# Band transposes over three PSUM banks, one block's output norm moved into the output projection, and token rows squared on the chip instead of loaded again

## The chip, the cores and the metric

The kernel runs on one core of a Trainium2 chip. The metric is the device time of one execution in microseconds (us). The kernel before has a median of 3063.79 us over three runs (3062.14 to 3065.21).

## The reference

One layer of a hybrid streaming encoder, in float32, over 2048 prompt tokens and 32 sample tokens (`T` = 2080 together), 1024 channels each. Cut to what matters here:

```python
a = rmsnorm(x, g_attn)                       # mean of x*x over the 1024 channels
qa, ka, va, qb, kb, vb = split(a @ w_in)     # group A: 4 heads, group B: 8 heads of 64
oa = diff_attn(qa, ka, va)                   # two softmax maps, w = p1 - lam * p2
ob = band_attn(qb, kb, vb)                   # a chunk of 64 sees itself and 8 chunks before
oa = rmsnorm_per_head(oa, subln_g) * (1 - lam_init)
ob = rmsnorm(ob, out_norm_b)                 # over the 512 channels of group B
h = x + concat(oa, ob) @ w_out
c = rmsnorm(h, g_mlp)
h = h + square(relu(c @ w_up)) @ w_down
h = h + sigmoid(h @ w_ple_gate) * (p @ w_ple_proj)
y = rmsnorm(h, g_final)
```

New keys and values of both groups are outputs too.

## The kernel before, in words

Every float32 operand of a large product is split into a high and a low part (`split`, lines 178 to 187), and `mm3` (lines 215 to 221) makes one product of three matmuls on TensorE (PE). So a group of 8 terms is 24 matmuls into one PSUM bank, which ScalarE (ACT) or VectorE (DVE) then empties ("evicts").

The tokens are cut into blocks b = 0 to 3 of 512, 512, 512 and 544 columns. The program is written as generators that are woven together, and a scheduler puts each engine's instructions into one fixed order when the program is built. Each engine then works through its own order, waiting wherever its next instruction isn't ready. All loads and stores are issued by one queue (SP), in order too. The written order of the first third is:

1. `prep` of blocks 0 and 1 beside the group A values (`vtile`, `vps`). For every 128 tokens `prep` loads the tokens transposed (`xt`, from `x_t`), multiplies by the gain, splits into `aH` and `aL`, loads the same tokens a second time as rows (`x`), squares these on ACT with a sum along the row (line 385), and makes the norm factor `r` from the sum (`rsqrt`). The values are scaled with `r` as they leave PSUM (`vraw`, line 427). `prep` of blocks 2 and 3 comes later, beside projections.
2. Group A queries and keys of blocks 0 and 1 (`proj`, `qps`), then the differential attention `attn_a` of the first half of the tokens, with the group B projections of all blocks as work to fill in.
3. Band attention `attn_b` of the first half (`JB[:2]`), 64 steps of 128 queries (8 heads, 4 pairs, 2 tiles each). A full step is four score matmuls `sb`, five transposes `tpb` of the softmax row, and three output matmuls `ob` (six for each pair of tiles); the first 32 steps see fewer keys and have two `sb`. Between `sb` and `tpb` lie additions and a maximum on DVE, an exponential on ACT, a reciprocal on DVE and a scaling on ACT. After `tpb`, ACT and DVE split the result into `pb`, which `ob` needs. Projections of blocks 2 and 3 in groups B and A (`proj_a`) are the filler here.
4. Band attention of the second half. Beside `proj_a`, `onorm` of blocks 0 and 1 is woven in: for each it loads the four band output tiles `oT` (`oraw`, a ring of three, tag `tmp`), squares and adds them (`sqacc`), sums over partitions with two matmuls (`css`, lines 1046 and 1047), makes the norm factor `r`, and stores it in DRAM (`rB`, line 1058).
5. `oload(0)`: eight raw tiles of block 0 are loaded through the same ring of three, tiles 4 to 7 are multiplied by `r`, which is loaded back from `rB` (`rb`, line 899), and all are split into the operands `oact` of the output projection.
6. The differential attention of the second half, then `outproj(0)` (`ops`, lines 918 to 925, eight steps d of eight terms) with `oload(1)` woven in, one tile for each d, then `outproj(1)`, then the MLP of blocks 0 and 1 (`ups`, `dps`) and so on.

PSUM has eight banks. Two (`mz`, tag `mm`) and a third (pool `mmx`) form the ring `mm` of the projections; `ps_s` has two for scores, `ps_t` two for transposes, `ps_o` one for outputs.

Of the kernel before, what the change touches and what calls it, by code (L numbers as in the profile page):

```python
# [20 lines left out]
P = 128  # L21
D = 1024
# [56 lines left out]
ONP = (28, 1, 6)  # L79
ONQ = (8, 1, 1)  # L80
PW = 272


def drain(gen):
    for _ in gen:
        pass
# [57 lines left out]
class Kern:  # L144
# [89 lines left out]
        eng.tensor_tensor(out, y0, v, op=ALU.mult)  # L234
        return out

    def xsrc(self, t0, n):
        a = self.a
        if t0 < SP:
            return a["x_prompt"][0, t0 : t0 + n, :]  # L240
        return a["x_sample"][0, t0 - SP : t0 - SP + n, :]

    def consts(self, cp):
        nc, a = self.nc, self.a
        self.ident = cp.tile([P, P], F32, name="ident")
        make_identity(nc, self.ident)
        ones = cp.tile([P, P], F32, name="ones")
        nc.gpsimd.memset(ones, 1.0)
        self.ones = cp.tile([P, P], F32R, name="ones_r")
        nc.vector.tensor_copy(self.ones, ones)  # L250

        def cols(name, ap, k):
            t = cp.tile([P, k], F32, name=name)
# [110 lines left out]
    def prep(self, b, acts, pp, mm, tag, first=None):  # L364
        nc = self.nc
        aH, aL = acts[b]
        late = []
        for i, (c0, n) in enumerate(toks(b)):
            t0 = 512 * b + c0
            xt = pp.tile([P, 8, P], F32, tag="xt", name="xt")  # L370
            self.dma(xt[:, :, :n], self.xT[:, :, t0 : t0 + n])
            if first is not None:
                first()
                first = None
            x = pp.tile([P, D], F32, tag="x", name="x")
            self.dma(x[:n], self.xsrc(t0, n))
            m = 2 if b == 0 and i == 0 else 1
            for k in range(0, 8, 8 // m):
                ks = slice(k, k + 8 // m)
                xg = xt[:, ks, :n]  # L380
                g = self.g_attn[:, ks].unsqueeze(2).broadcast_to([P, 8 // m, n])
                nc.vector.tensor_tensor(xg, xg, g, op=ALU.mult)
                self.split(aH[:, ks, c0 : c0 + n], aL[:, ks, c0 : c0 + n], xg, "act", "dve")
            st = pp.tile([P, 1], F32, tag="st", name="st")
            nc.scalar.activation(x[:n], x[:n], AF.Square, accum_out=st[:n])
            r = self.rcol[:n, 4 * b + i : 4 * b + i + 1]
            self.rsqrt(pp, st[:n], 1, 1.0 / D, EPS, nc.vector, "r1", n, out=r)

            def spread(r=r, c0=c0, n=n):
                nc.tensor.transpose(rp[:, c0 % 512 : c0 % 512 + n], r.broadcast_to([n, P]), self.ident[:n, :n])  # L390
# [474 lines left out]
        self.dma(t, self.oT[:, k, t0 : t0 + n])  # L865
        return t

    def onorm(self, b, wk, ps, tag, dst):
        nc = self.nc
        n, t0 = BN[b], 512 * b  # L870
        sq = wk.tile([P, BLK], F32, tag="acc", bufs=2, name="sqacc")[:, :n]
        for k in range(4, 8):
            raw = self.raw_o(wk, k, t0, n)
            if k == 4:
                nc.scalar.activation(sq, raw, AF.Square)
            else:
                nc.scalar.activation(raw, raw, AF.Square)
                self.pool_tt(sq, sq, raw, ALU.add)
        yield from self.colnorm2(sq, b, 1.0 / 512, wk, ps, tag, dst, [])

    def oload(self, b, wk, up, out):
        nc = self.nc
        n, t0 = BN[b], 512 * b
        if isinstance(up, tuple):
            oact = up[0].tile([P, 8, n], F32R, tag="h", name="oact")
            oact = [
                [oact[:, k] for k in range(8)],
                [up[1].tile([P, up[1].aw], F32R, tag="u", name="ou") for _ in range(8)],
            ]
        elif up.whole:  # L890
            oact = [up.tile([P, 8, up.aw], F32R, tag="act", name="oact") for _ in range(2)]
            oact = [[t[:, k, :n] for k in range(8)] for t in oact]
        else:
            oact = [[up.tile([P, up.aw], F32R, tag="u", name="ou")[:, :n] for k in range(8)] for _ in range(2)]
        out[b] = oact
        for k in range(8):
            if k == 4:
                r = wk.tile([P, BLK], F32, tag="r", bufs=2, name="rb")[:, :n]
                self.dma(r, self.rB[:, t0 : t0 + n])
            raw = self.raw_o(wk, k, t0, n)  # L900
            if k >= 4:
                nc.vector.scalar_tensor_tensor(
                    raw, raw, self.g_b[:, k - 4 : k - 3], r, op0=ALU.mult, op1=ALU.mult
                )
            self.split(oact[0][k], oact[1][k], raw, "act", "dve")
            yield
# [473 lines left out]
    def run(self):  # L1380
        tc, nc, a = self.tc, self.nc, self.a
        with ExitStack() as top:
# [91 lines left out]
            for js in JB[len(JB) // 2 :]:  # L1474
                self.attn_b(js, bp, ps_s, ps_t, ps_o)

            def proj_a():
                yield from self.proj(HALVES[1], 0, acts, sg, mm, gs=range(GS))
                for b in HALVES[1]:
                    yield from self.proj((b,), 0, acts, sg, mm, vs=(), gs=range(GS, 4))  # L1480
# [178 lines left out]
```

## Time and profile before

| | |
|---|---|
| median of three runs | 3063.79 us (3062.14 to 3065.21) |
| the profiled execution | 3069.65 us |
| its span | 3067.9 us |
| granted TensorE clock, mean | 0.985 |
| busy share PE, DVE, ACT, POOL | 96%, 60%, 57%, 62% |
| bytes moved by DMA | 529.54 MB, 173 GB/s over the span |

The profiled execution lies 5.86 us (0.19%) above the median of the timed runs, and its span is 1.75 us shorter than its time. PE is the busiest engine, so time is to be found where PE is not busy or where its clock is below 1.

### The profile page before, as it was taken

The page shows a single profiled execution, that of the slowest core. Times are in us where ns is not written, and L with a number is a line of the kernel's source. Part 1 is how long each engine was busy: PE and PEld are TensorE (multiplying, and loading weights), DVE is VectorE, ACT ScalarE, POOL GpSimd, SP SyncE. Part 2 cuts the span into 40 slices and gives each one's busy share as a digit, 9 for nine tenths or more (in the row PEclk, how much of TensorE's full clock was granted, in tenths as well). Part 3 has the DMA queues.
Part 4 walks back from the last instruction along what each step waited for, and adds up shares of the span by engine and source line. Part 5 has one row for each costly group of instructions (what it writes and reads, how often), then busy time and mean ns, then how long its engine had stood idle before and what let it go on. Part 6 is the DMA issues. An engine that isn't in the chain of part 4 may idle for free. (4 is left out here: it accounts for less than half of the span.)

```text
span 3067.9 us, 50404 instructions
## 1 busy us (share of the span) xinstructions
PE 2947.2 (96%) x17409; PEld 2599.0 (85%) x17409; DVE 1830.6 (60%) x4233; ACT 1746.5 (57%) x3234; POOL 1887.9 (62%) x2509
## 2 busy tenths in 40 slices
PE   7999999899789999999999999999899999999997
PEld 6788889899677888888888888879798888999997
DVE  5156554654655555566666565545677885577664
ACT  5256554765666666566666565554555545555455
POOL 3467775324146544656655565777688888787774
PEclk9999999999899999999999999999999999999999
DMA  9878866976687554455655543347433446333331
GB/s 310 250 222 245 241 221 211 262 228 211 190 248 241 147 148 131 145 155 172 198 149 155 150 128 125 118 148 249 136 131 117 148 151 231 122 101 112 102 99 57
DMA packets 298119, 529.54 MB, mean 173 GB/s; under 512 B 36668, under 2 KB 161632, under 8 KB 297864
## 3 DMA queue, kind: packets, MB, share of 16 engines
q1 hardware_dynamic: 297864, 526.32, 55.6%
q8 instruction: 138, 2.26, 0.3%
q14 instruction: 117, 0.96, 0.1%
HBM read 425.19 MB, written 104.97 MB: 173 GB/s over the span
## 5 line engine op out<-in xcount | busy, mean ns | idle before, releaser
L176 POOL TENSOR_TENSOR wl<-wr,wh 128x256 fp32r<-128x256 f32 x648 | 492.8, 792 | 270.2 <-ACT wh L181 230.7
L181 ACT ACTIVATE piece<-wr 128x512 fp32r<-128x512 f32 x406 | 245.8, 625 | 290.4 <-PE ups L220 133.3
L176 POOL TENSOR_TENSOR piece<-wr,piece 128x256 fp32r<-128x256 f32 x404 | 338.0, 863 | 92.3 <-ACT piece L181 85.2
L181 ACT ACTIVATE wh<-wr 128x1024 fp32r<-128x1024 f32 x228 | 240.5, 1055 | 190.8 <-PE ups L220 45.9
L166 POOL TENSOR_TENSOR wl<-wr,wh 128x256 fp32r<-128x256 f32 x264 | 202.9, 799 | 208.4 <-ACT wh L181 202.6
L219 PE MATMUL dps<-uh,piece 128*128 128x272 f32 (+1 forms) x768 | 247.0, 325 | 8.3 <-ACT piece L181 5.0
L221 PE MATMUL dps<-uh,piece 128*128 128x272 f32 (+1 forms) x768 | 247.3, 325 | 1.1 <-POOL piece L166 0.9
L220 PE MATMUL dps<-ul,piece 128*128 128x272 f32 (+1 forms) x768 | 248.1, 324 | 0.1
L166 POOL TENSOR_TENSOR piece<-wr,piece 128x256 fp32r<-128x256 f32 x280 | 235.1, 872 | 18.9 <-ACT piece L181 15.4
L219 PE MATMUL ups<-cs,piece 128*128 128x256 f32 (+1 forms) x864 | 246.2, 285 | 0.0
L221 PE MATMUL ups<-cs,piece 128*128 128x256 f32 (+1 forms) x864 | 246.1, 285 | 0.0
L220 PE MATMUL ups<-cs,piece 128*128 128x256 f32 (+1 forms) x864 | 245.9, 285 | 0.0
L219 PE MATMUL qps<-aH,wh 128*128 128x512 f32 (+1 forms) x640 | 226.9, 355 | 2.0 <-DVE ql L475 2.0
L220 PE MATMUL qps<-aL,wh 128*128 128x512 f32 (+1 forms) x640 | 227.9, 356 | 0.0
L221 PE MATMUL qps<-aH,wl 128*128 128x512 f32 (+1 forms) x640 | 226.5, 354 | 0.0
L1112 DVE TENSOR_TENSOR h<-h,dps 128x512 f32<-128x512 f32 x256 | 173.5, 682 | 80.2 <-PE dps L221 77.0
L638 ACT ACTIVATE e<-e,nm 128x128 f32<-128x128 f32 (+16 forms) x136 | 157.2, 1156 | 108.5 <-DVE nm L636 108.0
L1155 DVE TENSOR_TENSOR h<-h,dps 128x272 f32<-128x272 f32 (+1 forms) x384 | 189.0, 514 | 42.9 <-PE dps L221 42.3
L219 PE MATMUL dps<-uh,wh 128*128 128x512 f32 x512 | 205.7, 402 | 0.6 <-DVE h L1112 0.6
L219 PE MATMUL ups<-cH,wh 128*128 128x512 f32 x512 | 202.5, 396 | 0.0
L221 PE MATMUL ups<-cH,wl 128*128 128x512 f32 x512 | 202.2, 395 | 0.1
L220 PE MATMUL ups<-cL,wh 128*128 128x512 f32 x512 | 202.0, 394 | 0.0
(307 smaller groups left out, 9234.0 us busy)
## 6 DMA issues: line engine op xcount, KB each, us to landing
wr<-w_up SPq DMA_DIRECT2D x128, 512.0 KB, 3.5
wr<-w_down SPq DMA_DIRECT2D x128, 512.0 KB, 3.6
v<-vSa SPq DMA_DIRECT2D x64, 512.0 KB, 4.6
q<-qS SPq DMA_DIRECT2D x128, 256.0 KB, 5.2
wr<-w_qk SPq DMA_DIRECT2D x50, 512.0 KB, 5.2
ka<-kS SPq DMA_DIRECT2D x32, 512.0 KB, 7.1
wr<-w_out SPq DMA_DIRECT2D x32, 512.0 KB, 4.8
wr<-w_ple_gate SPq DMA_DIRECT2D x32, 512.0 KB, 3.5
```

The lines of the kernel that those rows point to most:

```text
L166: nc.gpsimd.tensor_tensor(out[:, sl], a[:, sl], b[:, sl], op=op)
L176: nc.gpsimd.tensor_tensor(out[:, sl], a[:, sl], b[:, sl], op=op)
L181: nc.scalar.activation(hi, raw, AF.Copy)
L219: nc.tensor.matmul(ps, lh, rh, start=start and i == 0, stop=False)
L220: nc.tensor.matmul(ps, lh, rl, start=False, stop=False)
L221: nc.tensor.matmul(ps, ll, rh, start=False, stop=stop and i == n - 1)
L638: nc.scalar.activation(row, row, AF.Exp, bias=nmx, accum_out=z[:nr, m : m + 1])
L1112: nc.vector.tensor_tensor(hv, hv, ps, op=ALU.add)
L1155: nc.vector.tensor_tensor(hv, hv, ps, op=ALU.add)
```

## The change: three edits to the first third of the program

**Transposes.** For the first half of the band attention the transposes `tpb` take their PSUM tile from a ring `tb` of three banks, the two of `ps_t` and the third bank `third`. The projections that run there (`proj` of blocks 2 and 3, `prep(3)`, `proj_a`) have the two banks of `mz` left. The second half of the band attention, and everything else that uses `mm`, is as before.

**Output norm.** `onorm(1)` is taken out of the weave with `proj_a`. Its two steps run inside `outproj(0)`, at d = 3 and d = 5, and `oload(1)` follows from d = 5 on, three tiles for each d. Its four raw tiles come in one load of 1 MB (`oraws`) into room of the pool that later holds `h`. For blocks 0 and 1 `r` stays in SBUF (`ro`); it isn't stored to `rB` and loaded again.

**Tokens.** The rows `x` are not loaded. The product with the gain goes to a tile of its own (`xg`), ACT squares `xt` in place, DVE adds up the eight channel groups (`sk`, reading with a step of 128 elements), and one matmul with a column of ones (`sp`) finishes the sum.

```diff
@@ def consts
+        self.one = ones[:, :1]
@@ def prep
-            x = pp.tile([P, D], F32, tag="x", name="x")
-            self.dma(x[:n], self.xsrc(t0, n))
+            xg = pp.tile([P, 8, P], F32, tag="xg", name="xg")
             m = 2 if b == 0 and i == 0 else 1
             for k in range(0, 8, 8 // m):
                 ks = slice(k, k + 8 // m)
-                xg = xt[:, ks, :n]
                 g = self.g_attn[:, ks].unsqueeze(2).broadcast_to([P, 8 // m, n])
-                nc.vector.tensor_tensor(xg, xg, g, op=ALU.mult)
-                self.split(aH[:, ks, c0 : c0 + n], aL[:, ks, c0 : c0 + n], xg, "act", "dve")
-            st = pp.tile([P, 1], F32, tag="st", name="st")
-            nc.scalar.activation(x[:n], x[:n], AF.Square, accum_out=st[:n])
+                nc.vector.tensor_tensor(xg[:, ks, :n], xt[:, ks, :n], g, op=ALU.mult)
+                self.split(aH[:, ks, c0 : c0 + n], aL[:, ks, c0 : c0 + n], xg[:, ks, :n], "act", "dve")
+            nc.scalar.activation(xt[:, :, :n], xt[:, :, :n], AF.Square)
+            sk = pp.tile([P, P], F32, tag="sk", name="sk")[:, :n]
+            nc.vector.tensor_reduce(sk, xt[:, :, :n].rearrange("p k c -> p c k"), axis=AX.X, op=ALU.add)
+            sp = mm.tile([P, 512], F32, tag=tag, name="sp")
+            nc.tensor.matmul(sp[:n, :1], sk, self.one, start=True, stop=True)
             r = self.rcol[:n, 4 * b + i : 4 * b + i + 1]
-            self.rsqrt(pp, st[:n], 1, 1.0 / D, EPS, nc.vector, "r1", n, out=r)
+            self.rsqrt(pp, sp[:n, :1], 1, 1.0 / D, EPS, nc.vector, "r1", n, out=r)
@@ def onorm
-    def onorm(self, b, wk, ps, tag, dst):
+    def onorm(self, b, wk, ps, tag, dst, out=None, room=None):
...
+            room, sq = room
+            sq = sq.tile([P, sq.aw], F32, tag="u", name="sqacc")[:, :n]
+            room = room.tile([P, 8, n], F32, tag="h", name="oraws")[:, :4]
+            self.dma(room, self.oT[:, 4:8, t0 : t0 + n])
         for k in range(4, 8):
-            raw = self.raw_o(wk, k, t0, n)
+            raw = self.raw_o(wk, k, t0, n) if room is None else room[:, k - 4]
...
-        yield from self.colnorm2(sq, b, 1.0 / 512, wk, ps, tag, dst, [])
+        yield from self.colnorm2(sq, b, 1.0 / 512, wk, ps, tag, dst, [] if out is None else out)
@@ def oload
-            if k == 4:
+            if k == 4 and r is not None:
+                r = r.pop()
+            elif k == 4:
                 r = wk.tile([P, BLK], F32, tag="r", bufs=2, name="rb")[:, :n]
                 self.dma(r, self.rB[:, t0 : t0 + n])
@@ the program
-            mm = Rings((mz, "mm"), (mz, "mm"), (opened(mmx, "mmx", 1, PSUM), "mm"))
+            third = opened(mmx, "mmx", 1, PSUM)
+            mm = Rings((mz, "mm"), (mz, "mm"), (third, "mm"))
...
+            tb = Rings((ps_t, "tp"), (ps_t, "tp"), (third, "mm"))
             for js in JB[: len(JB) // 2]:
-                self.attn_b(js, bp, ps_s, ps_t, ps_o)
-            weave(self.proj((2,), 1, acts, sg, mm), lifted(self.prep(3, acts, pp, mm, "mm")), 3)
+                self.attn_b(js, bp, ps_s, tb, ps_o)
+            weave(self.proj((2,), 1, acts, sg, mz), lifted(self.prep(3, acts, pp, mz, "mm")), 3)
...
-            drain(self.proj((3,), 1, acts, sg, mm))
+            drain(self.proj((3,), 1, acts, sg, mz))
...
-            weave2(proj_a(), [self.onorm(b, wq, mm, "mm", self.rB) for b in HALVES[0]], ONP)
+            ro = {b: [] for b in HALVES[0]}
+            weave2(proj_a(), [self.onorm(0, wq, mm, "mm", None, ro[0])], ONP)
...
-            drain(self.oload(0, wq, actq, oa))
+            drain(self.oload(0, wq, actq, oa, ro[0]))
...
-            weave(self.outproj(0, wk, oa[0], mm, acc[0]), self.oload(1, wk, (hq, uq), oa), 1, 0, OW)
+            g = self.onorm(1, wk, mm, "mm", None, ro[1], (hq, uq))
+            for i, _ in enumerate(self.outproj(0, wk, oa[0], mm, acc[0])):
+                if i in (O1, O2):
+                    next(g, None)
+                if i == O2:
+                    g = self.oload(1, wk, (hq, uq), oa, ro[1])
+                if i >= O2:
+                    for _ in range(O3):
+                        next(g, None)
+            drain(g)
```

In `proj_a` the ring `mm` becomes `mz` too; `O1, O2, O3 = 3, 5, 3`.

The scheduler makes a new order of this. The first place is TensorE at the last projection matmul (`qps`). Of before, in the order of the engine, with the line ahead and the shape behind:

```order
L221 MATMUL qps<-aH,wl 128x272
L1046 MATMUL css<-sh,ones_r 128x512
L1047 MATMUL css<-sl,ones_r 128x512
L804 MATMUL sb<-kbt,q 128x320 x4
L856 MATMUL ob<-pb,vbt 128x512 x4
L856 MATMUL ob<-pb,vbt 128x2x128
L826 MATMUL tpb<-ident,eb 128x128 x4
```

The last `qps` stands behind 176 `sb` of the band attention. From there full steps of four `sb` follow one another with nothing between them, until the first matmul of the output projection, behind 224 `sb`. These are the rows there, also of before:

```order
L804 MATMUL sb<-kbt,q 128x320 x4
L826 MATMUL tpb<-ident,eb 128x128 x4
L219 MATMUL ops<-oact,wh 128x512 x2
L826 MATMUL tpb<-ident,eb 128x128
L220 MATMUL ops<-oact,wh 128x512
```

So twelve full steps stand without a matmul of other work. The same two places of the changed kernel fit into one piece of the order of TensorE:

```order
L823 MATMUL tpb<-ident,eb 128x128 x5
L221 MATMUL qps<-aL,wh 128x272
L222 MATMUL qps<-aH,wl 128x272
L1051 MATMUL css<-sh,ones_r 128x512
L1052 MATMUL css<-sl,ones_r 128x512
L801 MATMUL sb<-kbt,q 128x320 x4
L853 MATMUL ob<-pb,vbt 128x512 x4
L853 MATMUL ob<-pb,vbt 128x2x128
L823 MATMUL tpb<-ident,eb 128x128 x4
L853 MATMUL ob<-pb,vbt 128x2x128
L823 MATMUL tpb<-ident,eb 128x128
L220 MATMUL ops<-oact,wh 128x512 x2
```

Now the last `qps` stands behind 240 `sb`, 16 full steps later than before, and the first `ops` behind 244: the output projection follows one step behind the last projection. The first 36 `ops` use raw tiles 0 to 3 of three steps d, which need no norm. The first `ups` of the MLP stands behind 296 `sb` before and behind 316 now, which is five full steps.

The second place is the queue SP at the start of the program, first of before:

```order
L157 DMA xt<-x_t 128x8x128
L157 DMA g_attn_s<-g_attn 128x8
L157 DMA x<-x_prompt 128x1024
L157 DMA wr_142<-w_v 128x1024
L157 DMA wr_151<-w_v 128x1024
```

and of the changed kernel:

```order
L158 DMA xt<-x_t 128x8x128
L158 DMA g_attn_s<-g_attn 128x8
L158 DMA wr_144<-w_v 128x1024
L158 DMA wr_153<-w_v 128x1024
L158 DMA xt<-x_t 128x8x128
```

The loads of weights and of the next tokens move up by the loads of rows, 17 in all. On DVE 17 instructions `sk` are new, on TensorE 17 matmuls `sp`. From about 2050 us of the profile on, the orders of PE and DVE are the same.

More of the change, by code (lines that the diff above doesn't have):

```diff
@@ L81 @@
 PW = 272
+O1, O2, O3 = 3, 5, 3
 def drain(gen):
@@ L235, in rsqrt @@
         return out
[L237 to L241, printed above, removed]
     def consts(self, cp):
@@ L866, in raw_o @@
         return t
-    def onorm(self, b, wk, ps, tag, dst):
+    def onorm(self, b, wk, ps, tag, dst, out=None, room=None):
         nc = self.nc
         n, t0 = BN[b], 512 * b
-        sq = wk.tile([P, BLK], F32, tag="acc", bufs=2, name="sqacc")[:, :n]
+        if room is None:
+            sq = wk.tile([P, BLK], F32, tag="acc", bufs=2, name="sqacc")[:, :n]
+        else:
+            room, sq = room
+            sq = sq.tile([P, sq.aw], F32, tag="u", name="sqacc")[:, :n]
+            room = room.tile([P, 8, n], F32, tag="h", name="oraws")[:, :4]
+            self.dma(room, self.oT[:, 4:8, t0 : t0 + n])
         for k in range(4, 8):
-            raw = self.raw_o(wk, k, t0, n)
+            raw = self.raw_o(wk, k, t0, n) if room is None else room[:, k - 4]
             if k == 4:
@@ L878, in onorm, with oload @@
                 self.pool_tt(sq, sq, raw, ALU.add)
-        yield from self.colnorm2(sq, b, 1.0 / 512, wk, ps, tag, dst, [])
-    def oload(self, b, wk, up, out):
+        yield from self.colnorm2(sq, b, 1.0 / 512, wk, ps, tag, dst, [] if out is None else out)
+    def oload(self, b, wk, up, out, r=None):
         nc = self.nc
@@ L1477, in proj_a @@
             def proj_a():
-                yield from self.proj(HALVES[1], 0, acts, sg, mm, gs=range(GS))
+                yield from self.proj(HALVES[1], 0, acts, sg, mz, gs=range(GS))
                 for b in HALVES[1]:
-                    yield from self.proj((b,), 0, acts, sg, mm, vs=(), gs=range(GS, 4))
-            weave2(proj_a(), [self.onorm(b, wq, mm, "mm", self.rB) for b in HALVES[0]], ONP)
+                    yield from self.proj((b,), 0, acts, sg, mz, vs=(), gs=range(GS, 4))
+            ro = {b: [] for b in HALVES[0]}
+            weave2(proj_a(), [self.onorm(0, wq, mm, "mm", None, ro[0])], ONP)
             s12.close()
@@ L1630 @@
     arrays["ck_t"] = np.ascontiguousarray(np.stack(ck).transpose(0, 3, 2, 1)).reshape(2, P, 512)
-    arrays["x_t"] = columns(arrays["x_prompt"][0], arrays["x_sample"][0])
+    arrays["x_t"] = columns(arrays.pop("x_prompt")[0], arrays.pop("x_sample")[0])
     arrays["p_t"] = columns(arrays.pop("p_prompt")[0, 0], arrays.pop("p_sample")[0, 0])
```

## The prediction

> **What bounds the kernel now.** I read the shares of the engines first, then windows over the stretches that the change touches, then what TensorE (PE) waits for, then single waits in the timeline.
>
> ```profile
> PE 2947.2 (96%) x17409; PEld 2599.0 (85%) x17409; DVE 1830.6 (60%) x4233; ACT 1746.5 (57%) x3234; POOL 1887.9 (62%) x2509
> ```
>
> PE is busy 2947.2 of 3067.9 us, so the kernel's time is PE's work plus its gaps and slow stretches. The windows (length, then busy time and count of PE, PEld, DVE, ACT, POOL, then PE's granted clock, the DMA share and GB/s) show where these lie:
>
> ```profile
> 0.00:50.00 50.00, 27.68 (x175) 25.32 (x175) 33.29 (x64) 33.26 (x72) 27.98 (x35) 0.97 1.01 348
> 50.00:100.00 50.00, 49.78 (x312) 42.77 (x313) 20.16 (x70) 19.83 (x53) 3.69 (x6) 0.97 0.70 221
> 130.00:170.00 40.00, 40.00 (x170) 32.28 (x169) 4.75 (x7) 8.24 (x11) 22.15 (x32) 0.98 0.67 219
> 520.00:773.00 253.00, 242.79 (x1690) 227.04 (x1689) 132.12 (x496) 160.18 (x359) 90.44 (x150) 0.99 0.80 233
> 773.00:825.40 52.40, 35.29 (x149) 26.46 (x148) 29.16 (x109) 33.91 (x71) 7.26 (x15) 0.77 0.66 192
> 825.40:965.00 139.60, 126.09 (x606) 103.54 (x606) 80.40 (x224) 85.44 (x161) 68.22 (x99) 0.97 0.83 241
> 1000.00:1200.00 200.00, 200.00 (x1015) 167.75 (x1014) 107.35 (x361) 131.94 (x263) 97.29 (x149) 1.00 0.51 148
> ```
>
> Three stretches stand out: the start; 773 to 825.4 us (PE at 67% and clock 0.77), between the last `qps` and the first `ops`; and the output projection behind it. What PE works on is counted by tile: `ops` in 825.4:965, then `sb`, `ups` and `dps` in 1000:1200.
>
> ```profile
> 825.40:965.00 139.60, 98.16 (x383) 0.97 0.83 241
> 1000.00:1200.00 200.00, 27.21 (x128) 1.00 0.51 148
> 1000.00:1200.00 200.00, 75.57 (x300) 1.00 0.51 148
> 1000.00:1200.00 200.00, 82.47 (x326) 1.00 0.51 148
> ```
>
> **Two prices.** In 130:170 PE does 170 matmuls of 512 columns without a gap, 40/170 = 0.235 us each (the durations of single ones overlap, so I use the spacing). In 1000:1200 it is full too: 626 such matmuls of the MLP and 128 `sb`, which at four each are 32 full band steps. A step that runs beside filler thus costs PE (200 − 626 × 0.235)/32 = 1.65 us.
>
> In 773:825.4 there are only the twelve full steps that the order shows without other work: 12 × 1.65 = 19.8 us of work in 52.4 us. 32.6 us are lost, since a step alone is a chain through DVE and ACT. In 825.4:965 there are 383 `ops`, 90.0 us, and 18 steps, 29.7 us: 119.7 of 139.6, 20 us lost.
>
> Why does the output projection start only at 825.4? The timeline of ACT, SP and PE just before it (start, duration, engine):
>
> ```profile
> 817.84 0.46 SPq L157 DMA_DIRECT2D oT<-t  x1
> 820.09 1.28 SPq L157 DMA_DIRECT2D oraw<-oT  x3
> 822.80 0.63 ACT L877 ACTIVATE oraw<-oraw 128x512 f32<-128x512 f32 x1 [1.13 <-DMA oraw<-oT]
> 824.52 1.14 ACT L181 ACTIVATE oact<-oraw 128x512 fp32r<-128x512 f32 x2
> 825.46 1.20 PE L219 MATMUL ops<-oact,wh 128*128 128x512 f32 x2
> ```
>
> Block 1's norm squares its last raw tile (L877) at 822.8, which could only be loaded after the last head's store `oT<-t` at 817.84. Block 0's raw tiles use the same ring of three and the same queue, so they stand behind it: block 0 waits for block 1.
>
> **Change 1 and 2, the middle of the program.** Taking `onorm(1)` out ahead of `oload(0)` removes that wait, and the new order puts `ops` one step behind the last `qps`. That `qps` itself stands 16 full steps later, as transposes have a third bank and projections one less. From 520 to 965 us it was 253 + 52.4 + 139.6 = 445 us. Now the first stretch holds 16 more steps, 16 × 1.65 = 26.4; one step follows, 1.65; then a wait T for block 0's norm; and the output projection sees five steps fewer before the first `ups` than the same point did, −8.25. 253 + 26.4 + 1.65 + T + 139.6 − 8.25 = 412.4 + T, a gain of 32.6 − T.
>
> T: the chain from `css` to the operands, as it was before:
>
> ```profile
> L1046 PE MATMUL css<-sh,ones_r x1: 394/394/394, 773.2 to 773.2; 128*128 128x512 f32 x1
> L157 SPq DMA_DIRECT2D rB<-r x1: 319/319/319, 784.2 to 784.2; - x1
> L902 DVE SCALAR_TENSOR_TENSOR oraw<-oraw,g_b_s,rb x8: 722/752/762, 835.1 to 911.2; 128x512 f32<-128x512 f32 x8
> L181 ACT ACTIVATE oact<-oraw x16: 613/624/636, 783.7 to 911.9; 128x512 fp32r<-128x512 f32 x16
> L187 DVE TENSOR_TENSOR oact<-oraw,oact x8: 669/678/694, 825.2 to 845.9; 128x512 fp32r<-128x512 f32 x8
> ```
>
> `r` is there 11.0 us after `css`; scaling and splitting tile 4 take 0.75 + 0.62 + 0.68. PE covers this with 36 `ops` (8.5 us) and one step (1.65): T = 2.9 at least. ACT and DVE work through band steps in between. The longest wait of that kind in this stretch bounds it from above; its rows are the matmul before it and the two that ended it:
>
> ```profile
> 863.79 0.39 PE L219 MATMUL ops<-oact,wh 128*128 128x512 f32 x1
> 869.92 0.63 ACT L181 ACTIVATE oact<-oraw 128x512 fp32r<-128x512 f32 x1 [7.11 <-DMA oraw<-oT]
> 872.77 0.76 PE L219 MATMUL ops<-oact,wh 128*128 128x512 f32 x1 [6.33 <-DVE stb L813]
> ```
>
> ACT stood 7.11 us for a raw load, and PE 6.33 us. T is 2.9 to 9.2; I take 6. After the wait one matmul took 0.76 us instead of 0.39, so a wait costs more than its length. The Trainium skill, page "TensorE: Matmul & The Clock Gate", section "Part 1: The HAM clock gate", says that an idle window of about 3.4 us halves PE's clock and that about as much busy time restores it; the 0.76 beside 0.39 agrees. By that rule a T of 6 would cost an estimated 1.7 us more, and the sum would be 1.7 us smaller.
>
> The moved norm is new work inside the output projection: a 1 MB load, four squares, a second `css` chain, and raw tiles of block 1 three at a time from d = 5 instead of one for each d. They stand in SP's and ACT's order ahead of weights and of the band steps' exponentials. Cover is the 24 matmuls of each d, 5.6 us. With it the price is 0, with two waits as above 12.7; I take 5, about one wait.
>
> The attention that is now denser before 520 I take at 0 (−8 to +10). Its row is that band steps there wait on DVE or are waited for, and either engine may gain from the third bank:
>
> ```profile
> PE sb L804 <- DVE stb L807: 16.9, 17, 2.2
> L475 DVE SCALAR_TENSOR_TENSOR ql<-qps,rbt x40: 422/677/693, 90.2 to 766.9; 128x512 f32<-128x512 f32 x24, 128x272 f32<-128x272 f32 x16
> ```
>
> With two banks a projection group can begin while the other is emptied. The eviction takes 0.68 us and a group of 24 matmuls 5.6 us, so the third bank isn't needed as long as DVE comes to it in time.
>
> **Change 3, the start.** All 16 DMA engines are full in 0:50 (share 1.01, 348 GB/s). PE is idle 22.3 us, 10.1 of them ahead of its first matmul:
>
> ```profile
> PE vps L219 <- ACT wh L181: 10.1, 1, 10.1
> PE vps L219 <- ACT vraw L427: 9.2, 4, 4.3
> L385 ACT ACTIVATE x<-x x17: 1039/1048/1062, 7.7 to 94.4; 128x1024 f32<-128x1024 f32 x16, 32x1024 f32<-32x1024 f32 x1
> L385 ACT ACTIVATION_READ_ACCUMULATOR x<-x x17: 180/186/192, 8.6 to 95.4; 128x1 f32 x16, 32x1 f32 x1
> DMA x<-x_prompt: 17.9, 5
> L382 DVE TENSOR_TENSOR xt<-xt,g_attn_s x18: 685/1224/1809, 5.7 to 391.9; 128x1024 f32<-128x1024 f32 x15, 128x512 f32<-128x512 f32 x2, 128x256 f32<-128x256 f32 x1
> L390 PE MATMUL rp<-ident,rcol x17: 237/273/477, 14.7 to 448.0; 128*128 128x128 f32 x16, 32*128 32x32 f32 x1
> ```
>
> ACT stood idle 17.9 us for the row loads (524 KB, 1.5 us each at 348 GB/s). Without them weights and tokens land earlier and the squares start from data already there. What can be won is the 12.2 us after the first matmul and the 1.5 us of one load ahead of it. New is DVE's sum `sk` over 128x1024 numbers: no such row exists, the nearest is the product with the gain, same size, 1.22 us. Eight of them raise DVE from 33.3 to 43 of 50 us, so DVE becomes the next limit. I take 8 us of gain (0 to 13.7). The square costs as much as before, 1.05, less the 0.19 of the read.
>
> Nine `sk` and `sp` come later, where PE is full: 17 × 0.273 = 4.6 us is the most for all `sp`, by the transposes `rp`, and nothing the least if they fall into gaps; I take 3, waits included.
>
> **The sum.** 32.6 − 6 − 5 + 8 − 3 = 26.6 us. The profiled execution took 3069.65 us and would take 3043.0; it lay 5.86 us above the median of the timed runs, so I predict 3037.2.
>
> **The rivals.** *The sum `sk` is slow.* Its reads step by 512 bytes, which no vector instruction of this trace shows. If each took twice 1.22 us, eight would add 19.6 us to 33.3, above the 50 us of the window: the start would lose about 3 us instead of winning 8, and the time would be 3048. The Trainium skill, page "SBUF — State Buffer", section "Door 1: The DMA port swizzle", speaks for it: accesses that cross to a new 16-byte line each pay a penalty, and it names four float32 as the stride that is free. No run shows it here; the chance is 0.12.
>
> *All of it comes back.* T and the norm are hidden, and the 10.2 us idle in 520:773 go with the third bank: 26.6 + 11 + 10.2 = 47.8, 3016 us. For it: the short waits of `sb`. Against: the chain of 11 us. 0.1.
>
> *Two banks starve the projections.* Blocks 2 and 3 have 84 groups of projections. If 40 waited for a whole eviction, 40 × 0.68 = 27 us would cancel the gain: 3064. For it: DVE's order now holds more transposes' work beside them. Against: 5.6 us of cover. 0.12.
>
> *The slower side: ACT blocks on block 1's loads.* ACT works in order, and in the new order squares and splits of block 1 stand between exponentials and weight splits. Each late load gives PE a wait of 6.33 us. The DMA share over 825.4:965 is 0.83 already, and one such wait is there. The gain is gone after 26.6/6.33 = 4.2 of them beyond those counted; with five it is 3069. Nine loads come in question. Against it: eight such loads brought one such wait before. 0.1.
>
> **The numbers.** The forecast as worked out has 0.5; 0.06 remain for what I don't see. A measurement of this kernel tells about 0.2% (6 us) from no change. Faster: 0.5 + 0.12 + 0.1, 0.05 of the starved case and 0.03 of the rest, 0.80. Same: 0.05, the starved case in the middle. Slower: 0.15. The range 3011 to 3062 takes in the forecast with its bounds (T, the start, the denser attention), the slow sum, the full recovery and half of the starved case, and leaves out the slower side.
>
> **What would show it.** After: PE about full, clock near 1, between the last `qps` and the first `ops`, with a wait of 3 to 9 us for tile 4; the first `ups` 26.6 − 8.25, some 18 us, earlier with five more steps behind it; PE idle in 0:50 down by some 8 us; `sk` at about 1.2 us. The prediction is wrong if PE waits for projection evictions (`ql`, `vraw`) between 400 and 820 us, if `sk` takes over 2 us, or if ACT stands for `oraws` or `oraw` more than twice.

## The result, and the profile after

The changed kernel takes 3052.11 us (median, 3048.17 to 3059.83) beside 3065.21 us before; the ratio is 0.996, interval 0.9948 to 0.9972. It is faster, but by 13.1 us where 26.6 were forecast. Run again on another occasion it gave 0.9962 (0.9948 to 0.9976). Two things came out, and in part they cancel: the middle of the program won about 8 us more than forecast, and the token part, forecast to win 5 us, lost about 18.

The profiled execution of the changed kernel has a span of 3058.0 us. It was the slowest of its seven executions, so I read places in it, not its total. First the same windows as before (length, busy time and count of PE, PEld, DVE, ACT, POOL, PE's granted clock, DMA share, GB/s):

```profile
0.00:50.00 50.00, 32.10 (x197) 30.27 (x198) 42.49 (x51) 27.79 (x47) 29.84 (x35) 0.93 0.82 250
50.00:100.00 50.00, 46.50 (x291) 38.58 (x291) 17.73 (x55) 11.22 (x25) 5.03 (x8) 0.96 0.56 178
773.00:825.40 52.40, 52.01 (x328) 47.00 (x327) 30.11 (x100) 36.77 (x73) 25.11 (x38) 1.00 0.84 252
825.40:965.00 139.60, 124.94 (x590) 101.86 (x589) 80.01 (x222) 87.13 (x161) 79.05 (x111) 0.96 0.82 243
```

The hole at 773 is gone: 328 matmuls instead of 149, clock 1.00 instead of 0.77. The start has changed its limit, as the prediction said, from DMA (share 1.01, now 0.82) to DVE (33.3, now 42.5 us). But PE has not done more for it by 100 us: 487 matmuls before (175 + 312), 488 now (197 + 291), and 16 of these are the short `sp`. DVE was forecast at 43 us. Not forecast was that this is too much already, since it is not spread evenly. Here are the 20 us from 30 to 50, of before and of the changed kernel, and then the sums `sk` alone in the first 50 us of the changed kernel:

```profile
30.00:50.00 20.00, 9.99 (x66) 8.94 (x64) 15.10 (x36) 14.66 (x38) 8.77 (x10) 0.91 1.08 378
30.00:50.00 20.00, 13.23 (x82) 12.42 (x81) 20.00 (x26) 9.56 (x19) 8.16 (x8) 0.84 0.71 210
0.00:50.00 50.00, 15.75 (x8) 0.93 0.82 250
```

From 30 to 50 us DVE has no gap at all. That the whole 50 us came out as forecast is a coincidence: the eight sums took 15.75 us and not 9.8, and 21 fewer of DVE's other instructions than before had run by then (43 of them beside the 8 sums, against 64). The groups by tile of the changed kernel show the new instruction (duration in ns least/median/most), and the product with the gain, of the same size, beside it:

```profile
L380 DVE TENSOR_REDUCE sk<-xt x17: 601/1986/2070, 8.3 to 417.7; 128x128 f32<-128x1024 f32 x16, 128x32 f32<-128x256 f32 x1
L376 DVE TENSOR_TENSOR xg<-xt,g_attn_s x18: 685/1214/1765, 5.3 to 401.9; 128x1024 f32<-128x1024 f32 x15, 128x512 f32<-128x512 f32 x2, 128x256 f32<-128x256 f32 x1
```

`sk` takes 1.99 us where 1.22 was assumed. In the middle the wait T for tile 4 was forecast at 6 us; the timeline shows it right behind the matmuls of tiles 0 to 3:

```profile
828.61 0.97 PE L220 MATMUL ops<-oact,wh 128*128 128x512 f32 x3
830.84 0.50 PE L221 MATMUL ops<-oact,wh 128*128 128x512 f32 x1 [1.27 <-DVE oact L188]
```

It is 1.27 us. What PE waited for in 825.4:965 (in total, times, longest):

```profile
PE ops L220 <- ACT wh L182: 5.1, 2, 4.8
PE ops L220 <- ACT oact L182: 4.4, 2, 2.7
PE sb L801 <- DVE stb L804: 3.3, 2, 2.1
PE ops L221 <- DVE oact L188: 1.3, 1, 1.3
```

These are 14.1 us in all; the same list of before had one wait of 6.3 us and smaller ones. So block 1's norm brought about as much waiting as it took away (13.4 us before).

### The profile page after: what moved, and what is told of

It is laid out like the page before. It is cut to its first block, busy times and chain, and to the rows that moved or that the text cites. A ratio compares the mean times of both kernels' runs of the same rounds, so it can differ in the third digit from the quotient of the medians.

```text
span 3058.0 us, 50401 instructions
## 1 busy us (share of the span) xinstructions
PE 2948.6 (96%) x17443; PEld 2600.5 (85%) x17443; DVE 1854.8 (61%) x4250; ACT 1744.1 (57%) x3217; POOL 1888.8 (62%) x2509
```

## Experiments: the three parts by themselves

Theory A, for the small gain: the sum `sk` on DVE is too long, and the token part eats what the middle wins. Theory B: the projections suffer from two banks, and the tokens are neutral. For the middle, A1: any work that fills the lone steps wins their time; A2: it is the moved norm that frees block 0. Each run was made beside the kernel before on the same chip. I compare by the ratio to it; times in the text are the ratio's distance from 1 by 3064 us, unless a median is named. An interval of 0.002 to each side of a ratio is 6 us.

**No token part.** `prep` as before, third bank and moved norm as in the change.

```diff
-            xg = pp.tile([P, 8, P], F32, tag="xg", name="xg")
+            x = pp.tile([P, D], F32, tag="x", name="x")
+            self.dma(x[:n], self.xsrc(t0, n))
...
-            nc.vector.tensor_reduce(sk, xt[:, :, :n].rearrange("p k c -> p c k"), axis=AX.X, op=ALU.add)
+            nc.scalar.activation(x[:n], x[:n], AF.Square, accum_out=st[:n])
```

> The changed kernel with the token rows loaded and squared as before: only the third bank and the moved norm are in. Theory A (the slow sum sk, 1.99 us each, and its matmuls eat the gain at the start and cost some 9 us from 100 to 520 us): about 10 us faster than the changed kernel, near 3041 us, and PE's gaps from 100 to 520 us about as before. Theory B (projections with two banks are what loses 9 us from 100 to 520 us, the tokens are neutral): the same time as the changed kernel, near 3052 us, with the gaps of that stretch still there.

3035.15 us, ratio 0.9902 (0.988 to 0.9925): 30 us faster than before and 18 faster than the whole change. Theory B falls.

**The token part alone.** The other side of the same edit, on the kernel before.

> The kernel before with the token part alone. Theory A: slower than before by 5 to 11 us (3070 to 3076 us), with DVE full from 30 to 50 us. Theory B: within 3 us of before. The prediction on record put this part at 5 us faster (8 at the start less 3 later).

3078.15 us, ratio 1.0049 (1.0031 to 1.0068): 15 us slower. The cost is the same size with and without the other parts, and above the range of Theory A.

**The third bank alone.**

```diff
+            tb = Rings((ps_t, "tp"), (ps_t, "tp"), (third, "mm"))
-                self.attn_b(js, bp, ps_s, ps_t, ps_o)
+                self.attn_b(js, bp, ps_s, tb, ps_o)
...
-            drain(self.proj((3,), 1, acts, sg, mm))
+            drain(self.proj((3,), 1, acts, sg, mz))
```

> The kernel before with the transposes on three banks and the projections on two, the norm of block 1 where it was. In the order the last qps moves behind 236 sb and the first ops behind 240. Theory A1 (the stretch of lone band steps is what cost time, the third bank alone fills it): some 15 to 25 us faster than before, with a wait for block 0's operands of 10 us or more ahead of the first ops. Theory A2 (block 0 waits for block 1 through the ring of raw tiles, so without the moved norm the filler only ends earlier against the same wait): under 8 us faster.

3043.59 us, ratio 0.9931 (0.9912 to 0.995): 21 us faster, Theory A1. But the wait that I put ahead of the first `ops` did not come. It starts at 797.9 us, as early as in the run without the token part (798.5), and ends later. The groups of `ops` in the kernel before, the third bank alone and the run without the token part (the last two numbers ahead of the shape are the first and the last start):

```profile
L219 PE MATMUL ops<-oact,wh x128: 387/391/775, 825.5 to 964.7; 128*128 128x512 f32 x128
L219 PE MATMUL ops<-oact,wh x128: 387/392/796, 797.9 to 948.7; 128*128 128x512 f32 x128
L220 PE MATMUL ops<-oact,wh x128: 387/393/632, 798.5 to 933.2; 128*128 128x512 f32 x128
```

So block 0's wait for block 1, which the prediction read from the timeline, was real in the old order, but the third bank removes it as well. Block 1's heads are complete with the 192nd `sb` (32 short steps of two, 32 full ones of four). Before, the last `qps` stood ahead of that, at 176; with the third bank it stands at 236, when block 1 has long been done. The moved norm is worth its 9 us on top (30 against 21) inside the projection: 134.7 us from first to last `ops` instead of 150.8, which holds one more step.

**The moved norm alone.** Banks as before.

```diff
-            weave2(proj_a(), [self.onorm(b, wq, mm, "mm", self.rB) for b in HALVES[0]], ONP)
+            weave2(proj_a(), [self.onorm(0, wq, mm, "mm", None, ro[0])], ONP)
...
```

> The kernel before with the norm of block 1 moved and r kept in SBUF, banks as before. In the order the last qps stays behind 176 sb and the first ops moves from behind 224 to behind 180, so the output projection becomes the filler of the lone steps. Theory A1: about 20 us faster than before, as the lone stretch goes whichever way it is filled. Theory A2 as well: 15 to 25 us faster, since it is this edit that frees block 0; then the third bank adds little to it, and the two edits are not additive.

3065.59 us, ratio 1.0004 (0.9992 to 1.0015): nothing. Both theories were wrong here. The output projection does start at 770.7 us and fills the hole, and the last of its matmuls starts 45.7 us earlier than before with eight steps (13.2 us) still to come, 32.5 us won. It is given back later, in part where the band attention ends and the differential attention of the second half begins. Windows of PE in the moved norm alone, around that place:

```profile
1200.00:1250.00 50.00, 50.00 (x250) 1.00 0.37 123
1250.00:1300.00 50.00, 40.47 (x177) 0.83 0.45 122
1300.00:1350.00 50.00, 50.00 (x261) 1.00 0.55 159
```

In the run without the token part the same change of attention is at 1200:1250, and it costs little:

```profile
1200.00:1250.00 50.00, 47.75 (x227) 1.00 0.53 147
```

PE does 177 matmuls in 50 us where its neighbours hold 250 and 261, and where the kernel before holds 232: some 13 to 20 us of work less at 0.235 us each. PE's longest waits there are 3.9 us for a row of the attention (`e`) and 2.7 us for the MLP's `relu`; ACT stands 4.0 us for a raw tile of another block's norm, ahead of that `relu`:

```profile
ACT oraw L884 <- DMA oraw<-oT: 4.0, 1, 4.0
```

The profiled execution is the fastest of this kernel's eleven, 6 us under their median, so it shows less loss than the usual one, and I can't place the rest. What is shown: the hole can be filled by either edit, and filling it by the moved norm alone wins nothing in the end (−21 us for the bank, +1 for the norm, together −30). That the shortage of filler moves to the next attention fits these windows; no run shows that this is all of the loss.

## Experiments: why the token part costs 18 us

Theory A stays: it is the length of the sum on DVE. Against it stands Theory C: it is the tiles of blocks 2 and 3, whose squares and norm factors were finished by 99 us before and now stand in the middle of the attention.

**The sum as three additions** of adjacent halves, with no stride.

```diff
-            nc.vector.tensor_reduce(sk, xt[:, :, :n].rearrange("p k c -> p c k"), axis=AX.X, op=ALU.add)
+            for k in (4, 2):
+                nc.vector.tensor_tensor(xt[:, :k, :n], xt[:, :k, :n], xt[:, k : 2 * k, :n], op=ALU.add)
+            nc.vector.tensor_tensor(sk, xt[:, 0, :n], xt[:, 1, :n], op=ALU.add)
```

> The changed kernel with the sum over eight channel groups as three additions of adjacent halves (512, 256 and 128 elements, all read with step 1) in place of the strided reduce. Theory A (the length of sk on DVE is what the token part costs): by the rows 0.69 for 512 elements and about half and a quarter of it for the others, 1.2 to 1.3 us for each tile instead of 1.99, so the start fills and the time falls by 5 to 10 us to 3042 to 3047 us. Theory C (not DVE's time but that squares, sums and norm factors of blocks 2 and 3 now stand in the middle of the attention, where before they were done by 98 us): within 3 us of the changed kernel.

3046.78 us, ratio 0.9938 (0.9926 to 0.995): 7 us of the 18 come back.

**The same reduce over adjacent elements.** The sums are those of other elements, so the norm factors are not the right ones; sizes and work are the same.

```diff
+            if n == P:
+                nc.vector.tensor_reduce(sk, xt.rearrange("p k c -> p (k c)").rearrange("p (c k) -> p c k", k=8), axis=AX.X, op=ALU.add)
...
```

> The changed kernel with the reduce over eight adjacent elements instead of eight 512 bytes apart, for the 16 full tiles: same sizes, same order, the sums are those of other elements. The stride by itself: if it is what makes sk 1.99 us, the reduce takes about 1.2 us here and the time goes the way of the run with three additions; if a reduce simply takes that long, it stays at 1.99 us and at 3052 us.

3046.42 us, ratio 0.9932 (0.9915 to 0.9948): 9 us back. Its instructions stand in the same order as those of the change on PE, DVE and ACT, so the difference is the reduce's length alone. The reduce itself:

```profile
L381 DVE TENSOR_REDUCE sk<-xt x16: 1203/1207/1220, 8.7 to 388.2; 128x128 f32<-128x1024 f32 x16
```

1.207 us against 1.986: the step of 512 bytes alone costs 0.78 us on each of 16 tiles, and the price that I had assumed is that of reads side by side. With that price the run is still 9 us behind the run without the token part (0.9932 against 0.9902).

**No sum at all.** The matmul `sp` reads the squares of one channel group, so the norm factors lack seven eighths of the sum.

```diff
-            sk = pp.tile([P, P], F32, tag="sk", name="sk")[:, :n]
-            nc.vector.tensor_reduce(sk, xt[:, :, :n].rearrange("p k c -> p c k"), axis=AX.X, op=ALU.add)
-            nc.tensor.matmul(sp[:n, :1], sk, self.one, start=True, stop=True)
+            nc.tensor.matmul(sp[:n, :1], xt[:, 0, :n], self.one, start=True, stop=True)
```

> The changed kernel with no sum on DVE at all: the matmul sp reads the squares of the first of the eight channel groups only, so seven eighths of the sum are left out. It shows what dropping the row loads is worth when DVE has no more to do than before. Theory A: the 8 us that the prediction put on the start appear, PE's gaps in 0 to 50 us fall from 26 to 18 us, and the time is 3027 to 3032 us, below the run that kept the row loads (3035). Theory C: no better than 3040 us, with the gaps of 200 to 450 us still there.

3029.27 us, ratio 0.9882 (0.9867 to 0.9896): 36 us faster than before and 24 faster than the whole change. The 6 us to the run with the row loads kept are within the two intervals. Its start, and that of the run without the token part:

```profile
0.00:50.00 50.00, 35.92 (x251) 34.09 (x252) 38.47 (x63) 31.82 (x56) 31.27 (x35) 1.00 0.83 260
50.00:100.00 50.00, 50.00 (x290) 41.42 (x289) 12.97 (x36) 9.42 (x20) 10.73 (x17) 1.00 0.76 245
0.00:50.00 50.00, 30.41 (x175) 28.28 (x175) 33.88 (x65) 33.32 (x72) 27.98 (x35) 0.87 1.01 349
```

With DVE free of the sum, PE does 251 matmuls in the first 50 us instead of 175, and 541 by 100 us instead of 492. Without the 16 short `sp` that is 33 more, an estimated 5 to 8 us of work at 0.14 to 0.235 us each. So at the start a gain of about the size is there that the prediction put on the row loads.

But this kernel is not the change less its sums. The scheduler made another order for it: its last `qps` stands behind 258 `sb` and its first `ops` behind 260, where the change and the run without the token part have 240 and 244. Its first `ops` starts at 805.3 us, 6.8 us after the 798.5 of the run with the row loads, with four more steps done (6.6 us): what it won at the start is gone by there. A good part goes in the attention. PE in 100:520, of the run without a sum, the whole change, and the run without the token part:

```profile
100.00:520.00 420.00, 409.45 (x2505) 1.00 0.74 226
100.00:520.00 420.00, 409.43 (x2454) 0.99 0.71 224
100.00:520.00 420.00, 414.82 (x2543) 1.00 0.76 236
```

PE is idle 10.6 us there without any sum on DVE, as in the whole change, and 5.2 us with the row loads. So the run has the time of Theory A and the gaps of Theory C, and its 24 us can't be put down to the sums (32.3 us of DVE's time in the change), since the order of the work differs too. Of the 18 us, 7 to 9 are shown to be the stride.

**The token part for blocks 0 and 1 alone**, with third bank and moved norm.

```diff
+            if b < 2:
                 ... the token part
+            else:
                 ... rows loaded and squared as before
```

> The changed kernel with the token part for blocks 0 and 1 alone; blocks 2 and 3 load and square their rows as before. It splits the 15 us that the token part costs. By the gaps of the runs so far the start loses 3 us against the run that kept all row loads (3035) and the stretch from 100 to 520 us loses the rest. Theory A (DVE's time, wherever it is): both places lose, 3040 to 3045 us here. Theory C (it is the later blocks, whose squares, sums and norm factors were done by 98 us before and now stand in the attention): 3036 to 3040 us here.

3035.28 us, ratio 0.9908 (0.9892 to 0.9923): 2 us from the run without it, which is no difference by the intervals: gain and cost at the start cancel.

**For blocks 2 and 3 alone** (`if b >= 2`).

> The other half: blocks 0 and 1 load and square rows as before, blocks 2 and 3 (nine tiles, nine sk) sum on the chip. Theory A: 3041 to 3045 us, about half of the cost for about half of the sums. Theory C: 3045 to 3050 us, nearly all of the cost, with PE's gaps from 100 to 520 us at 22 us or more against 14 in the run that kept all row loads.

3040.04 us, ratio 0.9928 (0.9916 to 0.9941): 8 us from the run without the token part. Both halves came out below what either theory had set for them. The place is the stretch with the first attention. Windows of PE there, of the run without the token part, blocks 0 and 1 alone, blocks 2 and 3 alone, and the whole change:

```profile
100.00:450.00 350.00, 345.19 (x1982) 1.00 0.78 242
100.00:450.00 350.00, 344.21 (x1956) 0.99 0.77 238
100.00:450.00 350.00, 339.99 (x1926) 0.99 0.73 225
100.00:450.00 350.00, 339.43 (x1923) 0.99 0.74 229
```

With the later tiles on the chip PE does some 56 matmuls less in the same 350 us. The squares of blocks 2 and 3 were finished by 96 us before, and now run from 268 to 403 us; ACT's square, DVE's sum, PE's `sp` and ACT's norm factor stand there in the engines' orders among the attention's work. The order of PE's matmuls differs between the two runs as well, from 200 to 500 us and again from 900 us on, and no run separates the one from the other. What PE waits for in 100:520 of the whole change:

```profile
PE vps L220 <- ACT wh L182: 3.5, 1, 3.5
PE s L620 <- DVE e L627: 3.0, 3, 1.6
PE vps L220 <- ACT rsv L227: 2.0, 1, 2.0
```

Without the token part no wait in that stretch is longer than 1.1 us.

**The sum on PE**, for blocks 0 and 1: eight short matmuls of the squares, nothing on DVE, rows for the other blocks.

```diff
-                sk = pp.tile([P, P], F32, tag="sk", name="sk")[:, :n]
-                nc.vector.tensor_reduce(sk, xt[:, :, :n].rearrange("p k c -> p c k"), axis=AX.X, op=ALU.add)
-                nc.tensor.matmul(sp[:n, :1], sk, self.one, start=True, stop=True)
+                for k in range(8):
+                    nc.tensor.matmul(sp[:n, :2], xs[:, k, :n], self.ones[:, :2], start=k == 0, stop=k == 7)
...
```

> Third bank and moved norm as in the change; for blocks 0 and 1 the rows are not loaded, and the sum goes to PE alone: ACT writes the squares in the matmuls' type to a tile of its own, and eight matmuls of two columns add the channel groups, with no sk on DVE. Blocks 2 and 3 load rows as before. Eight tiles of eight short matmuls are some 0.1 us each, 6 us on PE where it has 14 us of gaps left without a sum. Theory A: the start gains 5 to 9 us over the run that kept the row loads, 3026 to 3031 us. A rival: the short matmuls stand in PE's order and wait for squares, so the gain is lost there, 3035 us or more.

3041.39 us, ratio 0.993 (0.9918 to 0.9943): no gain. The matmuls cost PE more than forecast (all 64 in the first 100 us):

```profile
0.00:100.00 100.00, 9.77 (x64) 0.95 0.78 241
```

That is 9.8 us of busy time, 0.153 us each, against 6 expected. On average over these 100 us, at a clock of 0.95, a matmul of two columns costs as much as one of 256 (`vps` in the same window, next row, 0.143 us each).

```profile
0.00:100.00 100.00, 55.10 (x384) 0.95 0.78 241
```

Where PE runs full, both are shorter, and still much alike:

```profile
59.74 0.28 PE L222 MATMUL vps<-wh,aL 128*128 128x256 f32 x1
59.86 0.95 PE L389 MATMUL sp<-ones_r,xs 128*128 128x2 f32 x8
60.67 0.36 PE L220 MATMUL vps<-wh,aH 128*128 128x256 f32 x1
```

Eight `sp` take 0.81 us to the next matmul, 0.10 each, and a `vps` 0.12. So the price that was forecast holds where PE is full, and the surplus came elsewhere. The rival named ahead of the run, that the short matmuls wait for squares, fits the time but not the waits: PE's one wait of `sp` for squares in the first 110 us, 6.2 us, is its first of all, and the first wait of the run with row loads is 9.7 us. Why the run ends 8 us behind the run with rows, and not beside it, stays open; its profiled execution is the fastest of its five and doesn't show it.

**Do the halves add up?** 2 and 8 us are not 18, so four kernels ran once more on one chip: the whole change, the whole change with the unread token arrays still among its inputs (a change of places in memory), and both halves.

> The changed kernel again, beside the halves on one chip: 3049 to 3055 us if the sum that does not add up is real, 3045 or less if the distance between the earlier runs was between chips.

> The changed kernel with the two token arrays still handed to it, though nothing reads them. The halves of the token part cost 0 and 5 us by themselves and 15 us together. If the place of the other arrays in memory is part of that (the two halves still had the row arrays among their inputs, the change has not), this run is 5 us or more faster than the changed kernel; if it is the work and its order, the time is the same within 3 us.

> The token part for blocks 0 and 1 alone, again, beside the whole change: 3033 to 3039 us as before if the halves' times hold.

> The token part for blocks 2 and 3 alone, again, beside the whole change: 3037 to 3043 us as before if the halves' times hold.

The whole gave 0.9962 (0.9948 to 0.9976), with the arrays 0.9962 (0.995 to 0.9975), blocks 0 and 1 alone 0.9912 (0.9895 to 0.9929), blocks 2 and 3 alone 0.9932 (0.9916 to 0.9948). So the earlier times hold, and the inputs' place has no part in them. By the ratios alone it isn't certain that the halves fall short of the whole: they cost 10 to 12 us together, the whole 18, and the run without the token part, which all three are measured from, has an interval of some 7 us to each side. The traces show more. At the first `ops`, behind the same 244 `sb` and all projections in each order, most of it does add up:

```profile
L220 PE MATMUL ops<-oact,wh x128: 387/391/796, 817.1 to 955.6; 128*128 128x512 f32 x128
L220 PE MATMUL ops<-oact,wh x128: 387/392/796, 803.6 to 935.9; 128*128 128x512 f32 x128
L220 PE MATMUL ops<-oact,wh x128: 387/391/796, 807.6 to 942.9; 128*128 128x512 f32 x128
```

That is the whole change, blocks 0 and 1, blocks 2 and 3. Against 798.5 without the token part the halves are 5.1 and 9.1 us late there, together 14.2, and the whole 18.6. Later the halves win some back and the whole does not: at the last of these rows they are 2.7 and 9.7 behind 933.2, the whole 22.4. Some 4 of these 10 us are already there at the first `ops` (18.6 against 14.2), and idle time of that size shows by 100 us: from 50 to 100 us PE is busy 46.5 and 45.8 us in the two traces of the whole change, and 50.0 in those of either half. PE waits there for a norm factor (`rsv`, 1.4 us) and for a table (`t_table`, 2.1 and 1.3 us), which neither half shows. Where the other 6 come from, inside the output projection, stays open.

## Why the prediction was wrong

**The hole in the middle: right, and under-sized.** The last `qps` and the first `ops` stand where the order had them, PE is full between them at clock 1.00, and first and last `ops` without the token part are 27.0 and 31.5 us earlier than before. The last has five more steps done ahead of it, 8.25 us, so 39.8 us are won by then, where 32.6 − 6 − 5 = 21.6 were forecast. (The prediction words the 8.25 us as five steps fewer in the output projection. It holds 18 in both orders, 224 to 296 `sb` and 244 to 316; the five are done ahead of it, and the sum is right as a credit for them.) Two terms were too dear: T is 1.27 us in the change and 2.29 without the token part, not 6, both below the lower bound of 2.9, and the moved norm cost nothing, not 5: 134.7 us from first to last `ops`, 139.2 before, where 139.2 + 6 + 5 was forecast. That is 15.5 of the 18.2 us between; the rest is won ahead of the first `ops`. Some of the gain is lost later, since the median is 30 us ahead, not 40.

**Which edit does it: wrong.** The prediction credited the moved norm with freeing block 0 and the third bank with moving the fillers. The third bank does both by itself (21 us), the moved norm by itself nothing.

**The start: the step that failed.** "Eight of them raise DVE from 33.3 to 43 of 50 us, so DVE becomes the next limit. I take 8 us of gain (0 to 13.7)." Without any sum PE is ahead by about that much at 100 us, so the row loads are worth it there. The step took the sums as free as long as DVE's average stayed below 50, though. The average hid 20 in 20 us from 30 to 50 us, and PE had done no more by 100 us than before; the 42.5 us that agree with the forecast agree by luck. By themselves the first two blocks end 2 us behind the row loads, so the term was 8 and measured −2.

**The later tiles: the second term mis-sized.** "Nine `sk` and `sp` come later, where PE is full … I take 3." They cost 8 to 9 us alone. The price counted PE's matmuls and left out that squares and norm factors, formerly done by 99 us, now stand in order amid the attention's work on ACT and DVE. That this, and not the other order of PE's matmuls that came with it, makes the 8 us is argued, not shown. The two terms are off by 10 and 5 to 6 us; with both in one kernel the token part costs 18 us where a gain of 5 was forecast, and some 6 to 8 us of that appear in neither half.

**The rivals.** *The sum is slow* named a right cause, with a chance of 0.12 and a time of 3048 (3052 measured), but about half of the mechanism; its time came out near only because the middle won more and the later tiles lost more than it says. The Trainium skill, page "SBUF — State Buffer", section "Door 1: The DMA port swizzle", says that accesses crossing to a new 16-byte line each pay a penalty; the rows agree, 1.99 us with a step of 512 bytes against 1.21 side by side, so it is a factor of 1.65, not the 2 that I took. The stride explains 7 to 9 of the 18 us, though; with a sum at full speed the token part still loses 9. *All of it comes back* is right for the wait T and the norm, which came out hidden, and wrong for the idle time before: PE is idle 9.4 us of 520:773 in the changed kernel, beside 10.2 before. *Two banks starve the projections* did not happen: the third bank alone wins 21 us. *ACT blocks on block 1's loads* happened, but cost little: from 700 to 965 us ACT stands four times for `oraw` and `oraws`, which the prediction had named as a sign of being wrong, but 6.7 us in all beside 19.0 before, and PE's waits for `oact` in 825.4:965 are 4.4 us in two. The other signs stayed away: PE waits 1.8 us for `ql` from 400 to 820 us, and `sk` takes 1.99 us, just below the 2 that were named. The first `ups` comes 5.7 us earlier in the change and 28.2 without the token part (965.4 before, 959.7, 937.2), where some 18 were forecast.

The fastest kernel here that computes the whole layer is the change without its token part, 3035.15 us (0.9902), with blocks 0 and 1 on the chip equal to it (3034.7 and 3035.28).

## What to carry to other kernels

A load that is dropped has to be weighed against the engine that makes up for it at its busiest 20 us, not over the window, and against the place in the order where the new work will stand: here work done early, before 100 us, came out cheaper than the same work amid the attention. Where a scheduler orders the whole program anew, an edit that only takes work out can change the order as well, so look at the order before a difference in time is put down to the edit. Where two edits fill the same hole, run each alone, since one of them may do most of it and the other may only move the hole to the next stage. A sum over an outer axis on VectorE was dearer by its stride here (1.99 us against 1.21); a halving tree of adjacent additions takes the stride away, but not the time of the adds.

## What the hardware showed that was not expected

A reduce of 128x1024 float32 takes 1.207 us when its eight terms lie side by side and 1.986 us when they lie 512 bytes apart. A contiguous reduce is as fast as a product of two tensors of that size (1.214 us). And a matmul of two columns keeps PE busy about as long as one of 256 (0.153 against 0.143 us on average in the first 100 us, 0.10 against 0.12 where PE is full), so short matmuls were no cheap way to add.
